# Loading the second query block's mixed heads ahead of the last pair's split

## The chip, the cores and the metric

The kernel runs on one core of a Trainium2 chip. A core has five engines with instruction streams of their own: TensorE (PE in the profile, with its weight loads as PEld), VectorE (DVE), ScalarE (ACT), GpSimd (POOL) and SyncE (SP), which here issues nearly all DMAs. The engines meet only at semaphores. The metric is the device time of one execution in microseconds, the median of several runs.

## The reference

The kernel computes one layer of an encoder over 2048 positions of width 1024 (in float32; `forgetting_attention` is a causal softmax over q k plus c[t] - c[s]):

```
h = rms_norm(x, norm_mix_g)
z = h @ w_in
out_a = spatial_gating(u_a, v_a, ...)             # 8 gMLP heads of 64, blocks of 128 positions
out_b = forgetting_attention(q_b, k_b, v_b, f)    # 8 attention heads of 64
x = x + concat([out_a, out_b]) @ w_out
x = x + conv_ffn(rms_norm(x), w_up, w_conv, b_conv, w_down)
out = rms_norm(x, norm_final_g)
```

What matters here is the third line from the bottom: the product with `w_out` needs, for each position, the 512 columns of the gMLP heads and the 512 columns of the attention heads. Together they are called the mixed heads.

## The kernel before, in words

Every large matmul is made of three: operands are split into a high part and a low remainder (hi, lo), and `mm3` (L210, its matmul is L216) adds hi x hi, hi x lo and lo x hi over 8 chunks of 128, 24 matmuls for one output tile of 128 x 512. In c_half the mixed heads are the stationary operand (`thi`, `tlo` in the profile) and `w_out` the moving one (`whi`, `wlo`), so these matmuls are listed as `mm<-whi,thi`, `mm<-wlo,thi` and `mm<-whi,tlo`.

The positions are worked on in four query blocks of 512 (0 to 3), two in each half of the sequence. Phase A (`a_half`) makes the projections and the gMLP heads and writes the transposed results to memory (`mixh`, `mixl`, one pair of arrays per block, rows 0 to 511). `c_half` multiplies the mixed heads of blocks 0 and 1 (its b = 0 and b = 1) with `w_out` and adds x; `d_half` is the first half of the feed-forward part; `c_late` and what follows do the same for blocks 2 and 3.

The attention is a filler that runs beside all of this. `b_stream` (L730) is a Python generator over 32 pieces, (head h, block tb), block by block. Every matmul of `mm3` counts a tick, and every few ticks `step` (L117) gives out the next small portion of the filler, with a priority 100 places ahead of its place in the program (AHEAD_B). `need(tb)` (L138) gives out portions until all pieces of the blocks up to tb are out. A piece is `b_max` (scores for the row maximum, L829 with the reductions L832 and L834 on DVE), then `b_mix` (scores again, L877 and L881, exponentials, product with the values, L865 and L866). After each second head `b_mix` divides the pair's output by the row sums (matmuls L916, four transposes L190 into a PSUM tile of tag `s`, product L923 into the tile `op`), splits it (`split_sb`: hi on ACT, L203, lo on DVE, L204) and writes it to rows 512 to 1023 of `mixh` and `mixl`, 128 rows for a pair. The scores and these transposes share the three PSUM tiles of tag `s` (`scores`, L787).

The mixed heads of a block are read back with `load_mix` (L936) into tiles of 4 chunks each: the first holds chunks 0 to 3 (the gMLP heads), the second chunks 4 to 7 (the attention pairs). Each load brings two chunks, 512 KB, hi and lo by turns. For block 1 there is one exception: the last pair, head 7 with tb = 1, is not written to memory but split straight into chunk 7 of the tiles (L925, L926). For that, `b_mix` gets the tiles itself with `parts(1)` (L172). `load_mix` then gets them as `given` and loads only chunk 6 in its last step (256 KB).

In `c_half` (L945) the order of the program for b = 0 is: four loads of x (`acc`), the weights and the four output tiles of column half 0, then `need(1)`, then `load_mix(1, self.mix1)`, which on SyncE comes behind the last `acc` load (`issue_after`), then the weights and output tiles of column half 1. Then comes b = 1 with the mixed heads of block 1.

Pieces with tb of 2 or more are held back until `self.ready` is set, since their inputs come late; before the change this happens in `run` (L1580), just ahead of `c_half`.

What order the engines get is not the program's: a planner (a list scheduler with its own model of time) places each instruction when its inputs and its buffer are there, by priority. Buffers come from pools, a fixed number per tag (`BUFS`: two `thi` and two `tlo` tiles per pool, one `op`, three `s`).

Of the kernel before, what the change touches and what calls it, by code (L numbers as in the profile page):

```python
# [33 lines left out]
AHEAD_B, AHEAD_W = 100, 2000  # L34
# [20 lines left out]
def f32(ap):  # L55
    return ap.bitcast(F32)
# [26 lines left out]
class Block:  # L83
# [51 lines left out]
    def start_fill(self, gen, rate):  # L135
        self.fill, self.rate, self.credit = gen, rate, 0.0

    def need(self, tb):  # L138

        while self.done < 8 * (tb + 1):  # L140
            self.step()
            self.count += 3
            while self.late and self.late[0][0] <= self.count:
                self.late.pop(0)[2]()
# [709 lines left out]
    def b_mix(self, h, tb, t1, turn):  # L854

        nc, bp, pp = self.nc, self.bp, self.bpp
        t2 = self.b_low(h, tb)
        po = self.til(pp, [P, TB], F32, "o")
        total = self.room([P, TB], F32, "sum")
        ns = 4 * tb + 4  # L860
        late = []

        def pv():
            sc, c, v, ph, pl = late.pop(0)
            nc.tensor.matmul(po[:, c], lhsT=v, rhs=ph[:, c], start=sc == 0, stop=False)  # L865
            nc.tensor.matmul(po[:, c], lhsT=v, rhs=pl[:, c], start=False, stop=sc == ns - 1)  # L866

        for sc in range(ns):
            if sc == TURN and turn:
                turn()  # L870
            if sc % 4 == 0:
                m1, m2, v4 = self.b_keys(h, sc // 4, True)
            j = max(0, sc - 4 * tb)
            c = slice(j * P, TB)
            ks = slice((sc % 4) * P, (sc % 4 + 1) * P)
            ps = self.scores([P, TB])
            nc.tensor.matmul(ps[:, c], lhsT=m1[:, ks], rhs=t1[:, c], start=True, stop=False)  # L877
            if sc >= 4 * tb and not tb:
                nc.tensor.matmul(ps[:, j * P:(j + 1) * P], lhsT=self.same, rhs=self.maskT, start=False, stop=False,
                                 skip_group_check=True)  # L880
            nc.tensor.matmul(ps[:, c], lhsT=m2[:, ks], rhs=t2[:, c], start=False, stop=True)  # L881
            if sc >= 4 * tb and tb:
                d = ps[:, j * P:(j + 1) * P]
                nc.vector.tensor_tensor(d, d, self.maskT, op=ALU.add)
            e = self.room([P, TB], F32, "e") if sc else total
            nc.scalar.activation(e[:, c], ps[:, c], AF.Exp, scale=-1.0)  # L886
            if len(late) >= (LAG + 1 if self.more else LAG):
                pv()
            ph = self.room([P, TB], F32R, "ph")
            pl = self.room([P, TB], F32R, "pl")  # L890
            nc.scalar.activation(ph[:, c], e[:, c], AF.Copy)  # L891
            nc.vector.tensor_tensor(pl[:, c], e[:, c], f32(ph[:, c]), op=ALU.subtract)  # L892
            if sc:
                nc.vector.tensor_tensor(total[:, c], total[:, c], e[:, c], op=ALU.add)  # L894
            late.append((sc, c, v4[:, sc % 4, :], ph, pl))
            yield
        while late:
            pv()
            yield

        if h % 2 == 0:
            self.op = self.til(self.mp, [P, TB], F32, "op")
            self.fold = self.til(self.mp, [P, TB], F32, "rw")
        op, fold = self.op, self.fold
        own, other = (slice(0, 64), slice(64, 128)) if h % 2 == 0 else (slice(64, 128), slice(0, 64))
        nc.scalar.activation(op[own, :], po[other, :], AF.Copy)
        nc.vector.tensor_tensor(op[own, :], po[own, :], op[own, :], op=ALU.add)
        nc.scalar.activation(fold[own, :], total[other, :], AF.Copy)
        nc.vector.tensor_tensor(fold[own, :], fold[own, :], total[own, :], op=ALU.add)
        if h % 2 == 0:  # L910
            return

        yield
        ps = self.scores([P, 4, 2])
        for i in range(4):
            nc.tensor.matmul(ps[:, i, :], lhsT=fold[:, i * P:(i + 1) * P], rhs=self.pair, start=True, stop=True)  # L916
        rr = self.til(bp, [P, 4, 2], F32, "rr")
        nc.vector.reciprocal(rr, ps)
        rw = self.til(self.mp, [P, 4, 2, 64], F32, "rw")
        nc.scalar.activation(rw, rr.unsqueeze(3).broadcast_to([P, 4, 2, 64]), AF.Copy)  # L920
        yield
        pr = self.transpose4(None, "s", [rw[:, i, :, :].rearrange("p a b -> p (a b)") for i in range(4)])
        nc.vector.tensor_tensor(op, pr, op, op=ALU.mult)  # L923
        if h == 7 and tb == 1:
            self.mix1 = self.parts(1)  # L925
            self.split_sb(op, *[part[:, 7, :] for part in self.mix1])  # L926
            return
        oh = self.room([P, TB], F32R, "ph")
        ol = self.room([P, TB], F32R, "pl")
        self.split_sb(op, oh, ol)  # L930
        cs = slice(512 + (h - 1) * 64, 512 + (h + 1) * 64)
        self.dma(self.mixh[tb][cs, :], f32(oh))
        self.dma(self.mixl[tb][cs, :], f32(ol))
# [11 lines left out]
    def c_half(self, half, accp):  # L945
        nc, pp = self.nc, self.dpp
        mix = [self.mix0, None]
        for b in range(2):
            mh, ml = mix[b]
            rows, acc = [], []  # L950
            for t in range(4 * b, 4 * b + 4):
                x = self.til(accp, [P, D], F32, "acc")
                t0 = half * HALF + t * P
                acc_ins = self.dma(x, self.a["x"][0, t0:t0 + P, :]).ins
                acc.append(x)
            for col in (b, 1 - b):
                if b == 0 and col == 1:
                    self.need(2 * half + 1)
                    with self.tc.issue_after(acc_ins):
                        mix[1] = self.load_mix(1, self.mix1)  # L960
                cs = slice(col * 512, (col + 1) * 512)
                if b == 0 or col == 0:
                    us = [self.load_unit(self.a["w_out"][4 * col + j], 512) for j in range(4)]
                    wh = [us[k // 2][0][:, k % 2, :] for k in range(KC)]
                    wl = [us[k // 2][1][:, k % 2, :] for k in range(KC)]
                for t in range(4):
                    ts = slice(t * P, (t + 1) * P)
                    ps = self.til(pp, [P, TB], F32, "mm")
                    self.mm3(ps, [mh[:, k, ts] for k in range(KC)], [ml[:, k, ts] for k in range(KC)], wh, wl)
                    ac = acc[t]  # L970
                    nc.vector.tensor_tensor(ac[:, cs], ps, ac[:, cs], op=ALU.add)
                    if col == 1 - b:
                        self.dma(self.rows_d[half][4 * b + t], ac)
                        row = self.til(self.rowp, [P, D], F32, "ar")
                        r = self.row_scale(self.dp, ac, row)
                        nc.gpsimd.tensor_scalar(row, ac, r, 0.0, ALU.mult, ALU.add)
                        rows.append(row)
            hi, lo = self.hT[b] = self.parts(b)

            def turn(c, rows=rows, hi=hi, lo=lo):  # L980
                self.transpose_split(pp, "dn", [r[:, c * P:(c + 1) * P] for r in rows],
                                     self.g_ffn[:, c:c + 1], hi[:, c, :], lo[:, c, :])

            for c in range(KC):
                self.defer(26 + 8 * c, lambda c=c, turn=turn: turn(c))
# [574 lines left out]
    def run(self):  # L1560
# [16 lines left out]
        self.dp = dstack.enter_context(tc.tile_pool(name="dpool", bufs=1, reuse_waits="tile"))  # L1577
        self.accs, self.bxs = ExitStack(), ExitStack()
        self.rowp = self.accs.enter_context(tc.tile_pool(name="rowp", bufs=1, reuse_waits="tile"))
        self.ready = True  # L1580
        self.rate = RATES[2]
        self.c_half(0, accp)
        self.rate = RATES[3]
# [51 lines left out]
```

## Time and profile before

| | us |
|---|---|
| median of 3 runs | 2375.96 (2373.01 to 2376.89) |
| the profiled execution | 2374.53 |
| its span, first to last instruction | 2372.8 |
| granted TensorE clock, mean | 0.998 |

The page's second part cuts the span in 40 slices of 59.3 us and gives the busy share of each in tenths:

```profile
PE   9999999999899999999999999999999999999998
DVE  7458777876679888999899986698888887866875
DMA  6763625568645444444444474222222238438633
```

TensorE shows 9 nearly everywhere. The one 8 in the middle, the eleventh slice, is 593 to 652 us, in which `c_half` lies. Busy means here that some matmul was in the array; since matmuls overlap (a matmul of 512 columns is listed with some 0.39 us and the next one begins 0.23 us later), a full slice doesn't say that the array ran at its best rate. The rows to read are therefore the idle times that stand in square brackets behind an instruction, with what ended them, and the distance between starts.

In the timelines a line is: start in us, duration, engine, line of the kernel, operation, output<-inputs, partitions and elements, count. For DMA issues on SyncE (SPq) the duration is that of issuing, not of the transfer. `x2` means that two issues in a row are shown as one.

### The profile page before, as it was taken

Reading aid. Unit: us, or ns where it says so; the run is one execution under the profiler, and the core shown is the slowest. Engines: PE = TensorE matmul, PEld = TensorE weight load, DVE = VectorE, ACT = ScalarE, POOL = GpSimd, SP = SyncE. Lnnn points to the kernel's source line nnn. Section 1 sums busy time; section 2 is a strip of 40 time slices with the busy share of each in tenths; the row PEclk is TensorE's granted clock in tenths of the full one; section 3 lists DMA queues with packets and bytes.
Section 4 is the critical chain, followed back from the end, with each engine's and each line's share of the span. In section 5 each row is a group of like instructions: output and inputs, shape, how many; then the busy total and the mean of one; then the engine's idle time right before and its main releaser. Section 6 shows DMA issues by size and latency. Waiting matters only on the chain.

```text
span 2372.8 us, 32085 instructions
## 1 busy us (share of the span) xinstructions
PE 2348.2 (99%) x11144; PEld 1957.7 (83%) x11144; DVE 1883.7 (79%) x3146; ACT 1215.6 (51%) x2189; POOL 281.3 (12%) x278
## 2 busy tenths in 40 slices
PE   9999999999899999999999999999999999999998
PEld 7988888988787888888888888788888888888887
DVE  7458777876679888999899986698888887866875
ACT  4346646533436555656566654555545555454444
POOL 4114140100223111111100101100000000000001
PEclk9999999999999999999999999999999999999999
DMA  6763625568645444444444474222222238438633
GB/s 213 197 227 113 191 87 168 156 191 269 219 144 205 165 149 143 148 164 165 150 146 149 151 244 147 93 71 80 80 81 98 80 133 292 147 124 291 199 114 125
DMA packets 232818, 374.29 MB, mean 158 GB/s; under 512 B 49784, under 2 KB 109304, under 8 KB 231232
## 3 DMA queue, kind: packets, MB, share of 16 engines
q1 hardware_dynamic: 227616, 348.12, 45.5%
q0 software_dynamic: 5040, 24.12, 2.6%
q8 instruction: 88, 1.44, 0.2%
q14 instruction: 74, 0.61, 0.1%
HBM read 279.10 MB, written 93.20 MB: 157 GB/s over the span
## 4 chain that ended last, share of the span: by engine, by line
PE 91%; DVE 4%; DMA 2%; issue 1%; ACT 1%; POOL 1%; SPq 0%; POOLq 0%; DVEq 0%; ACTq 0%
PE mm L216 43%; PE D L1449 15%; PE A L1247 3%; PE A L1249 3%; PE A L1248 3%; PE o L866 3%; PE o L865 3%; PE s L881 2%; PE s L877 2%; PE s L829 2%; PE B L1248 2%; PE B L1249 2%; PE B L1247 2%; PE C L1247 1%; PE C L1248 1%
## 5 line engine op out<-in xcount | busy, mean ns | idle before, releaser
L216 PE MATMUL mm<-thi,whi 128*128 128x512 f32 x896 | 351.4, 392 | 1.2 <-DVE vn L538 1.2
L216 PE MATMUL mm<-thi,wlo 128*128 128x512 f32 x896 | 351.8, 393 | 0.0
L216 PE MATMUL mm<-tlo,whi 128*128 128x512 f32 x896 | 351.8, 393 | 0.0
L216 PE MATMUL mm<-whi,thi 128*128 128x512 f32 (+2 forms) x768 | 275.5, 359 | 6.4 <-DMA thi<-mixh 5.0
L216 PE MATMUL mm<-wlo,thi 128*128 128x512 f32 (+2 forms) x768 | 274.7, 358 | 0.0
L216 PE MATMUL mm<-whi,tlo 128*128 128x512 f32 (+2 forms) x768 | 273.7, 357 | 0.0
L216 PEld LDWEIGHTS mm<-thi,whi 128*128 128x128 f32 x896 | 168.6, 188 | 36.0 <-POOL whi L152 1.1
L216 PEld LDWEIGHTS mm<-tlo,whi 128*128 128x128 f32 x896 | 168.5, 188 | 34.5
L216 PEld LDWEIGHTS mm<-thi,wlo 128*128 128x128 f32 x896 | 168.6, 188 | 34.1
L216 PEld LDWEIGHTS mm<-whi,thi 128*128 128x128 f32 x768 | 144.9, 189 | 26.5 <-DMA thi<-mixh 5.3
L169 DVE TENSOR_TENSOR wlo<-raw,whi 128x1024 fp32r<-128x1024 f32 (+2 forms) x106 | 132.5, 1250 | 40.1 <-POOL whi L152 24.6
L216 PEld LDWEIGHTS mm<-wlo,thi 128*128 128x128 f32 x768 | 145.0, 189 | 19.3
L216 PEld LDWEIGHTS mm<-whi,tlo 128*128 128x128 f32 x768 | 144.6, 188 | 19.4
L886 ACT ACTIVATE e<-s 128x512 f32<-128x512 f32 (+3 forms) x204 | 104.0, 521 | 90.9 <-PE s L881 50.2
L1006 DVE SCALAR_TENSOR_TENSOR t<-a,cols,t 128x512 f32<-128x512 f32 (+2 forms) x176 | 139.4, 792 | 11.7 <-ACT t L1000 10.9
L1449 PE MATMUL D<-wl,xh 128*128 128x512 f32 x368 | 141.3, 389 | 0.0
L1449 PE MATMUL D<-wh,xh 128*128 128x512 f32 x368 | 140.8, 389 | 0.2 <-DVE xo L1550 0.2
L1449 PE MATMUL D<-wh,xl 128*128 128x512 f32 x368 | 137.5, 389 | 0.0
L152 POOL TENSOR_SCALAR whi<-raw 128x1024 fp32r<-128x1024 f32 (+3 forms) x70 | 79.9, 1144 | 484.7 <-PE mm L216 360.7
L894 DVE TENSOR_TENSOR sum<-sum,e 128x512 f32<-128x512 f32 (+3 forms) x189 | 119.5, 632 | 17.1 <-ACT e L886 15.7
L892 DVE TENSOR_TENSOR pl<-e,ph 128x512 fp32r<-128x512 f32 (+3 forms) x189 | 115.4, 616 | 12.5 <-PE o L866 10.6
L891 ACT ACTIVATE ph<-e 128x512 fp32r<-128x512 f32 (+3 forms) x189 | 101.8, 548 | 28.4 <-PE o L865 13.7
(1931 smaller groups left out, 5749.0 us busy)
## 6 DMA issues: line engine op xcount, KB each, us to landing
raw<-in_w_up_dram SPq DMA_DIRECT2D x72, 512.0 KB
x<-act SPq DMA_DIRECT2D x84, 256.0 KB
m<-kx SPq DMA_DIRECT2D x67, 256.0 KB
v<-vd SPq DMA_DIRECT2D x67, 256.0 KB
m<-kx SPq DMA_DIRECT2D x119, 136.0 KB
raw<-in_w_in_dram SPq DMA_DIRECT2D x28, 512.0 KB
raw<-in_w_out_dram SPq DMA_DIRECT2D x24, 512.0 KB
tw<-in_w_down_dram SPq DMA_DIRECT2D x11, 1024.0 KB
```

What stands on the lines that cost most here:

```text
L152: self.cast_ins = self.nc.gpsimd.tensor_scalar(out, in_, 1.0, 0.0, ALU.mult, ALU.add).ins
L169: nc.vector.tensor_tensor(lo, raw, f32(hi), op=ALU.subtract)
L216: self.last_mm = self.nc.tensor.matmul(ps, lhsT=a[k], rhs=b[k], start=i == 0, stop=i == 3 * n - 1).ins
L886: nc.scalar.activation(e[:, c], ps[:, c], AF.Exp, scale=-1.0)
L891: nc.scalar.activation(ph[:, c], e[:, c], AF.Copy)
L892: nc.vector.tensor_tensor(pl[:, c], e[:, c], f32(ph[:, c]), op=ALU.subtract)
L894: nc.vector.tensor_tensor(total[:, c], total[:, c], e[:, c], op=ALU.add)
L1006: nc.vector.scalar_tensor_tensor(t[:, c], a[:, n + c.start:n + TB], cw[:, cc], t[:, c], op0=ALU.mult, op1=ALU.add)
L1247: mm(ps, lhsT=xh[:, ks], rhs=yh[:, k, :], start=fresh and k == 0, stop=False, **kw)
L1248: mm(ps, lhsT=xh[:, ks], rhs=yl[:, k, :], start=False, stop=False, **kw)
L1249: mm(ps, lhsT=xl[:, ks], rhs=yh[:, k, :], start=False, stop=k == 3, **kw)
L1449: nc.tensor.matmul(bank[t], lhsT=x[i][:, ts], rhs=w[k], start=fresh and j == 0 and i + k == 0, stop=last and i == 1, **kw)
```

## The change

`need` takes a second argument, how many pieces may still be missing. The last pair of block 1 no longer gets tiles and splits; it leaves a function, `last_pair`, that does the split into tiles given later. `c_half` gets the tiles and loads the other chunks at its start (behind the `acc` loads, after `need(1, 2)`, which leaves out the last two pieces). Where it loaded them before, it now gives out the split, with the filler's priority, and sets `ready`, which `run` no longer sets. So the pieces of block 2 are held back until that place.

```diff
-    def need(self, tb):
+    def need(self, tb, left=0):
 
-        while self.done < 8 * (tb + 1):
+        while self.done < 8 * (tb + 1) - left:
...
         if h == 7 and tb == 1:
-            self.mix1 = self.parts(1)
-            self.split_sb(op, *[part[:, 7, :] for part in self.mix1])
+            self.last_pair = lambda parts: self.split_sb(op, *[part[:, 7, :] for part in parts])
             return
...
+            if not b:
+                self.need(1, 2)
+                with self.tc.issue_after(acc_ins):
+                    mix[1] = self.load_mix(1, self.parts(1))
             for col in (b, 1 - b):
                 if b == 0 and col == 1:
-                    self.need(2 * half + 1)
-                    with self.tc.issue_after(acc_ins):
-                        mix[1] = self.load_mix(1, self.mix1)
+                    self.need(1)
+                    with self.tc.high_priority(AHEAD_B):
+                        self.last_pair(mix[1])
+                    self.ready = True
...
-        self.ready = True
         self.rate = RATES[2]
         self.c_half(0, accp)
```

## The prediction

> **What bounds the kernel now.** I began with the page's first part, then the waits of TensorE (PE), then the groups by line.
>
> ```profile
> PE 2348.2 (99%) x11144; PEld 1957.7 (83%) x11144; DVE 1883.7 (79%) x3146; ACT 1215.6 (51%) x2189; POOL 281.3 (12%) x278
> ```
> ```profile
> PE mm L216 <- DMA thi<-mixh: 5.0, 1, 5.0
> ```
>
> TensorE is busy 99% of the span, so time can only come from its own work, which this change leaves alone, or from the few places where it stands still. The second fence is the longest of these: one wait of 5.0 us, of a matmul of `mm3` (L216) for a load of mixed heads. I looked for its place in TensorE's timeline (start, us, line, out<-in, idle before).
>
> ```profile
> 633.71 0.82 PE L190 MATMUL dn<-ident,ar 128*128 128x128 f32 x6
> 634.37 0.60 PE L190 MATMUL s<-ident,rw 128*128 128x128 f32 x4
> 634.72 0.71 PE L829 MATMUL s<-m,t 96*128 96x512 f32 x2
> 636.11 0.49 PE L829 MATMUL s<-m,t 96*128 96x512 f32 x1 [0.67 <-DVE part L832]
> 636.92 1.01 PE L829 MATMUL s<-m,t 96*128 96x512 f32 x2 [0.32 <-DVE op L923]
> 638.16 0.96 PE L829 MATMUL s<-m,t 96*128 96x512 f32 x2
> 644.13 0.79 PE L216 MATMUL mm<-whi,thi 128*128 128x512 f32 x1 [5.01 <-DMA thi<-mixh]
> 646.00 0.63 PE L829 MATMUL s<-m,t 96*128 96x512 f32 x1
> 648.12 0.48 PE L216 MATMUL mm<-whi,tlo 128*128 128x512 f32 x1
> ```
>
> The 192 matmuls of b=0 in `c_half` (8 groups of 24) end before 633.71. The matmul at 644.13 is the first of b=1. Between them stand only transposes and the first scores of the third query block (L829). Then I read the same place in stretches (us, engines, granted clock, DMA share, GB/s).
>
> ```profile
> 633.70:639.10 5.40, 4.33 (x20) 2.39 (x18) 5.10 (x9) 2.83 (x6) 1.86 (x3) 1.00 0.59 185
> 639.10:644.10 5.00, 0.02 (x1) 0.00 (x0) 3.18 (x6) 0.50 (x1) 0.00 (x0) 0.69 1.01 376
> 644.10:648.10 4.00, 3.97 (x15) 3.38 (x16) 1.16 (x4) 0.58 (x1) 0.00 (x0) 0.54 1.05 343
> ```
>
> The granted clock falls to 0.69 in the wait and is 0.54 for 4.0 us behind it, so the wait costs more than its 5.0 us.
>
> What the matmul waits for stands in SyncE's timeline, in the chain of waits, and in two lists of DMA issues (584 to 590 us, then 637 to 641).
>
> ```profile
> 585.51 0.43 SPq L102 DMA_DIRECT2D thi<-mixh  x1
> 588.08 0.57 SPq L102 DMA_DIRECT2D tlo<-mixl  x1
> 592.32 7.71 SPq L102 DMA_DIRECT2D m<-kx  x3
> 637.20 1.72 SPq L102 DMA_DIRECT2D thi<-mixh  x2
> 639.47 1.13 SPq L102 DMA_DIRECT2D tlo<-mixl  x2
> ```
> ```profile
> 637.20 6.89 DMA thi<-mixh
> ```
> ```profile
> thi<-mixh SPq DMA_DIRECT2D x1, 512.0 KB
> thi<-mixh SPq DMA_DIRECT2D x1, 256.0 KB
> ```
> ```profile
> thi<-mixh SPq DMA_DIRECT2D x2, 512.0 KB
> ```
>
> The 256 KB piece is chunk 6 alone (`n = 1`), so the issues at 585 to 588 fill the second tile (chunks 4 to 6), and those at 637 to 640 the first (chunks 0 to 3). Chunks 0 to 3 are the gMLP heads, whose writes to memory end soon after 402 us (all 16, with first and last start):
>
> ```profile
> L102 SPq DMA_DIRECT2D mixh<-st x16: 359/374/492, 232.1 to 402.1; - x16
> ```
>
> They are late for another reason, which the next rows show (ACT, then DVE).
>
> ```profile
> 636.81 0.63 ACT L203 ACTIVATE thi<-op 128x512 fp32r<-128x512 f32 x1 [1.02 <-DVE op L923]
> ```
> ```profile
> 638.48 0.68 DVE L204 TENSOR_TENSOR tlo<-op,thi 128x512 fp32r<-128x512 f32 x1
> ```
>
> These are the last pair's split. The `thi` loads follow its ACT half by 0.39 us, the `tlo` loads its DVE half (ends 639.16) by 0.31. In program order the split is the first to write the second tile of each tag, and the load only later writes the first one. I read the rows so: the planner hands out a tag's tiles in program order of first use, so the first tile's loads are placed behind the split.
>
> **The change, part by part.** *The loads ahead of the split.* `parts(1)` and the loads now come ahead in program order, behind the four `acc` loads. So nothing holds chunks 0 to 3 any more, if their buffer is free:
>
> ```profile
> 575.10 0.39 PE L216 MATMUL mm<-thi,wlo 128*128 128x512 f32 x1
> ```
>
> This is phase A's last matmul out of that pool, ten us before the first load. So I put the four late issues at about 588.7, behind 588.08 + 0.57. On SyncE they take at most 1.72 + 1.13 = 2.85 us and pass only the `m<-kx` issue at 592.32, with 3.7 us free ahead of it: nothing is lost there. The DMA engines are another matter:
>
> ```profile
> 590.00:595.00 5.00, 5.00 (x24) 4.06 (x23) 4.68 (x8) 1.86 (x4) 0.00 (x0) 1.00 1.04 406
> 595.00:601.00 6.00, 6.00 (x31) 5.08 (x30) 5.04 (x9) 2.32 (x5) 1.42 (x2) 1.00 0.25 88
> ```
>
> They are full up to 595 at 406 GB/s. Four loads of 512 KB are 2.1 MB, 5.2 us at that rate; the next stretch has 0.75 x 6.0 = 4.5 us free. They spill over by 0.7 us and land by about 602, 32 us before b=1 needs them. At worst (no gap used) the attention filler's own loads land 5.2 us late; at best nothing moves. I take nothing, as the second row is the nearest.
>
> The Trainium skill (DMA: Bandwidth & Descriptors, Specifications) gives an HBM limit of about 358 GB/s per core and speaks against this cover: 2.1 MB would take 5.9 us and spill 1.4. The 406 GB/s of this trace is above that figure, so the measurement decides.
>
> *What is saved.* I count what TensorE did from 633.71 to 648.12, 14.41 us, and price it at full clock by rows of the chain of waits and two rows of the groups in this stretch:
>
> ```profile
> L829 PE MATMUL s<-m,t 96*128 96x512 f32 x8 | 3.8, 494 | 1.0 <-DVE part L832 0.7 <-DVE op L923 0.3
> L190 PE MATMUL dn<-ident,ar 128*128 128x128 f32 x16 | 3.0, 315 | 0.0
> ```
> ```profile
> 565.44 5.50 PE mm L216 x24
> 570.94 0.44 PE s L190 x4
> 571.38 0.47 PE s L829 x2
> ```
>
> Four L216 at 5.50/24 = 0.229 make 0.92; 16 + 4 transposes at 0.11 make 2.20; eight full L829 at 0.235 make 1.88, and two narrow ones (128 and 256 columns) some 0.2. Work 5.2, so **9.2 us are lost**: 5.01 + 0.67 + 0.32 = 6.0 in waits, the other 3.2 in the slow stretch and in issue.
>
> *The split behind the loads.* It adds a write behind landed loads: by 602 against 636.81, no wait. Behind it on ACT and DVE stand the transposed rows of b=0 (L199, L200), as now. What is late next is chunk 7: its low half is ready at 639.16. Even if TensorE goes straight to b=1 after the ten L190 at 633.71 (1.1 us), it reaches chunk 7 after 21 matmuls, 633.71 + 1.1 + 4.8 = 639.6. Cost nothing; if the filler is 5.2 us late, 4.8 us.
>
> *The third block waits.* `ready` is set 96 matmuls later in the program, so its pieces are given out later. This adds no semaphore. Its first scores (634.72) come behind the last pair's transposes (634.37), which use the same PSUM tag `s`, when all 192 matmuls of b=0 are done. So the later place already lies ahead of its execution: cost 0, with 96 x 0.229 = 22.0 us as the other end if the planner keeps the full distance. Below zero there is no gain, since it only moves work back.
>
> *The far end.* The last block's mixed heads are loaded as the filler ends. Timeline of SyncE, then the chain:
>
> ```profile
> 1473.04 0.37 SPq L102 DMA_DIRECT2D tlo<-mixl  x1
> ```
> ```profile
> 1481.12 1.83 PE mm L216 x8
> ```
>
> With the 6.89 us of the earlier load it lands at 1479.9 (an estimate). The first low-half matmul behind the transposes starts at about 1481, so the slack is some 1.0 us. The main work now arrives 9.2 us sooner. The filler gains too, since it stood behind the blocked matmul:
>
> ```profile
> 646.67 0.69 DVE L832 TENSOR_REDUCE part<-s 128x1 f32<-128x512 f32 x1 [4.39 <-PE s L829]
> ```
>
> DVE waited 4.39 us for the filler's next score. If the filler gains only that, the far end gives back 9.2 - 4.4 - 1.0 = 3.8 us; if it follows the main work, nothing. I take 1.3, nearer to nothing, because filler and main work share all engines and what is freed on DVE also speeds the filler.
>
> Sum: -9.2 + 1.3 = **-7.9 us**. The profiled execution took 2374.53 us (span 2372.8 and 1.7 around it), so 2366.6. The median of the runs, 2375.96, is 1.43 above that: **2368.1 us**.
>
> **The rivals.** *R1, the filler is late.* The moved loads hold up the filler's loads by 5.2 us, the split comes 4.8 us too late and b=1 waits for chunk 7. With about 2.0 us of slow clock behind it (4.0 us at 0.54 lose 1.8), 9.2 - 4.8 - 2.0 = 2.4 are saved: 2373.6. For it: DMA share 1.04 at 590. Against it: the 0.25 of the next row, and a second group's 21 matmuls that could run meanwhile.
>
> The Trainium skill (TensorE: Matmul & The Clock Gate, Part 1) says that an idle window of about 3.4 us halves the clock. The 0.69 and 0.54 above agree; by that rule R1's wait still pays for the slow stretch, and one under 3.4 us would not.
>
> *R2, given back at the far end.* The filler moves up by nothing: 9.2 - 1.0 = 8.2 are lost again at the last block, 2375.0. For it: the slack there is small. Against it: the 4.39.
>
> *R3, nothing changes.* The loads keep their place for a reason not seen, 2376.0. Against it: the free buffer, and the second tile's loads at 585.
>
> *R4, slower.* The third block really starts later, by d. Its end, and with it the load at 1473, moves back by d, and the last block waits: time = 2368.1 + d. From d = 7.9 the gain is gone. At the full 22.0, with 1.8 of slow clock, it is 2391.9. For it: the small slack at 1473. Against it: the order at 634.37 and 634.72.
>
> **How the numbers follow.** Forecast 0.65 (own range 2364 to 2371: the full 9.2, less 3 for the spread of the runs, and the 3.8 given back); R1 0.07; R2 0.10; R3 0.06; R4 0.12. The program is planned anew behind 585 us, which no row prices; it widens both ends. Range 2363.0 to 2376.5: it holds the forecast, R1, R2 and R3, 0.88, less 0.06 for tails. A measurement of this kernel can tell about 0.2%, 4.75 us, from no change. The forecast is faster (0.65), and a little of R1 and R2 (0.02); the rest of R1, R2 and R3 with the small d of R4 is the same (0.22); R4 beyond d = 12.7 slower (0.11).
>
> **What would show it.** Right: all `thi<-mixh` issues of this block below 592 us, no PE wait for `thi<-mixh` in the list of waits, granted clock 1.00 near 640, and the first L829 of the third block still behind the four transposes into `s`. R1: the split later than 640 us and a wait for `thi` or `tlo` from ACT or DVE. R2 and R4: a new wait of TensorE for `mixh` or `mixl` near 1470. Wrong altogether: the issues still at 637.

## The result, and the profile after

| | before | after |
|---|---|---|
| median, us | 2375.47 (6 runs, 2373.01 to 2376.89) | 2365.67 (6 runs, 2364.31 to 2368.37) |
| ratio | | 0.9959, 95% interval 0.9948 to 0.9969 |
| profiled execution, us | 2374.53 | 2365.29 |
| its span, us | 2372.8 | 2363.6 |

The change saves 9.8 us between the medians and 9.2 us between the spans; 2368.1 was predicted. The first part of the page and the longest of TensorE's waits, both after:

```profile
PE 2346.7 (99%) x11144; PEld 1957.6 (83%) x11144; DVE 1875.6 (79%) x3146; ACT 1216.0 (51%) x2189; POOL 282.3 (12%) x278
```
```profile
PE A L1251 <- ACT t2h L1092: 1.8, 1, 1.8
```

The wait for `thi<-mixh`, 5.0 us and the longest before, is gone from the list; the longest is now one of 1.8 us at another place (L1251). SyncE's timeline after shows the loads of block 1:

```profile
584.29 0.43 SPq L102 DMA_DIRECT2D thi<-mixh  x1
...
586.41 1.39 SPq L102 DMA_DIRECT2D thi<-mixh  x1
...
588.58 0.52 SPq L102 DMA_DIRECT2D thi<-mixh  x1
...
590.00 0.33 SPq L102 DMA_DIRECT2D thi<-mixh  x1
591.27 0.36 SPq L102 DMA_DIRECT2D tlo<-mixl  x1
592.57 5.95 SPq L102 DMA_DIRECT2D m<-kx  x3
```

All four `thi` loads stand ahead of 592 us, and the issue of `m<-kx` behind them has moved by 0.25 us (592.32 before). The same stretches of TensorE as in the prediction, and the two in which the loads were to fit (us, engines, granted clock, DMA share, GB/s), after:

```profile
595.00:601.00 6.00, 6.00 (x31) 5.08 (x30) 5.58 (x10) 2.09 (x5) 2.90 (x2) 1.00 0.96 351
601.00:606.00 5.00, 5.00 (x24) 4.17 (x23) 3.76 (x7) 1.36 (x3) 0.11 (x1) 1.00 0.91 290
633.70:639.10 5.40, 5.40 (x28) 4.44 (x28) 1.75 (x3) 0.99 (x3) 1.85 (x3) 1.00 0.61 179
639.10:644.10 5.00, 5.00 (x26) 4.08 (x25) 3.64 (x7) 1.38 (x2) 0.00 (x0) 1.00 0.69 224
644.10:648.10 4.00, 4.00 (x23) 3.38 (x22) 3.19 (x6) 1.36 (x2) 0.00 (x0) 1.00 0.42 156
```

From 633.70 to 648.10 TensorE is busy throughout, at full clock, with 28 + 26 + 23 = 77 instructions where before it had 20 + 1 + 15 = 36. The DMA gap at 595 is filled (0.96 where it was 0.25), and 601 to 606 is full as it was (0.91; 0.93 before).

So far this looks like a forecast that came out by its own reasons. The experiments show that it did so only in part: two of its steps failed, in opposite directions.

### The profile page after: what moved, and what is told of

Read it like the earlier page. It is cut to its first block, busy times and chain, and to the rows that moved or that the text cites. A ratio compares the mean times of both kernels' runs of the same rounds, so it can differ in the third digit from the quotient of the medians.

```text
span 2363.6 us, 32066 instructions
## 1 busy us (share of the span) xinstructions
PE 2346.7 (99%) x11144; PEld 1957.6 (83%) x11144; DVE 1875.6 (79%) x3146; ACT 1216.0 (51%) x2189; POOL 282.3 (12%) x278
## 4 chain that ended last, share of the span: by engine, by line
PE 83%; DVE 3%; DMA 2%; ACT 1%; issue 1%; POOL 0%; SPq 0%; POOLq 0%; DVEq 0%; ACTq 0%
PE mm L216 37%; PE D L1453 14%; PE A L1251 3%; PE A L1252 3%; PE A L1253 3%; PE o L866 3%; PE o L865 3%; PE s L881 2%; PE s L877 2%; PE s L829 2%; PE B L1253 2%; PE B L1252 2%; PE B L1251 2%; PE C L1252 1%; PE C L1253 1%
## 5 line engine op out<-in xcount | busy, mean ns | idle before, releaser
L216 PE MATMUL mm<-thi,whi 128*128 128x512 f32 x896 | 351.4, 392 | 0.5 <-DVE vn L538 0.5
L216 PE MATMUL mm<-thi,wlo 128*128 128x512 f32 x896 | 351.9, 393 | 0.0
L216 PE MATMUL mm<-tlo,whi 128*128 128x512 f32 x896 | 351.4, 392 | 0.0
L216 PE MATMUL mm<-whi,thi 128*128 128x512 f32 (+2 forms) x768 | 274.8, 359 | 2.3 <-DVE fs L536 1.4
L216 PE MATMUL mm<-wlo,thi 128*128 128x512 f32 (+2 forms) x768 | 274.4, 357 | 0.0
L216 PE MATMUL mm<-whi,tlo 128*128 128x512 f32 (+2 forms) x768 | 274.1, 357 | 0.0
L216 PEld LDWEIGHTS mm<-thi,whi 128*128 128x128 f32 x896 | 168.5, 188 | 35.0 <-issue 1.0
L216 PEld LDWEIGHTS mm<-thi,wlo 128*128 128x128 f32 x896 | 168.5, 188 | 34.7
L216 PEld LDWEIGHTS mm<-tlo,whi 128*128 128x128 f32 x896 | 168.5, 188 | 34.0
L216 PEld LDWEIGHTS mm<-whi,thi 128*128 128x128 f32 x768 | 144.7, 188 | 22.2 <-issue 1.5
L216 PEld LDWEIGHTS mm<-whi,tlo 128*128 128x128 f32 x768 | 144.6, 188 | 19.4
L216 PEld LDWEIGHTS mm<-wlo,thi 128*128 128x128 f32 x768 | 144.8, 188 | 19.2
L892 DVE TENSOR_TENSOR pl<-e,ph 128x512 fp32r<-128x512 f32 (+3 forms) x183 | 110.4, 607 | 20.8 <-PE o L866 10.9
L891 ACT ACTIVATE ph<-e 128x512 fp32r<-128x512 f32 (+3 forms) x183 | 98.4, 545 | 31.3 <-PE o L865 18.2
```

Source lines behind the costliest of these rows:

```text
L216: self.last_mm = self.nc.tensor.matmul(ps, lhsT=a[k], rhs=b[k], start=i == 0, stop=i == 3 * n - 1).ins
```

## The experiments

The question was which half of the edit makes the gain. Kernel 1 is that of experiment 1, and so on. The program of the third block matters for the answer, so here is the part that the prediction passed over. In `d_half`, behind its first two units, the kernel sets `self.more`. From that place in the program the filler has additional buffers (tags with a "+": `ph+`, `pl+`, `e+`, `m1+` and others), may put its scores also into PSUM tiles of tag `dn`, lets its products with the values lag one step more, and is given out woven: the scores of one head between the mixing steps of the head before it. From there ACT also makes the weights' casts, which GpSimd made before (L165). The place is fixed in the program, but how far the filler has come there depends on when `ready` was set.

### 1 and 2: each half alone

The loads ahead of the split, but the third block given out as early as before:

```diff
                     with self.tc.high_priority(AHEAD_B):
                         self.last_pair(mix[1])
-                    self.ready = True
...
+        self.ready = True
         self.rate = RATES[2]
         self.c_half(0, accp)
```

> The changed kernel, but with the third block's pieces given out as early as before the change (ready is set ahead of c_half); only the loads are moved. My theory (the whole gain is the wait for thi<-mixh with its slow stretch, and holding the third block back costs and gains nothing): as the changed kernel, 2365.7 us, within 2; chunks 0 to 3 loaded between 584 and 592 us, no wait of TensorE for thi<-mixh. Rival (the gain, or part of it, comes from holding the third block back): 2370 to 2375. Second rival (holding it back costs something that the gain covers): below 2363.

Measured: 2375.76 us, ratio to before 1.0000 (0.9991 to 1.0008). The loads alone gain nothing. The wait near 640 is gone in its profile too. In its place stands another, in the list of waits, in SyncE's timeline and in the stretches of the far end:

```profile
PE mm L216 <- DMA thi<-mixh: 6.4, 1, 6.4
```
```profile
1467.01 0.33 SPq L102 DMA_DIRECT2D mixh<-ph+_3176_13680  x1
...
1469.04 0.37 SPq L102 DMA_DIRECT2D thi<-mixh  x1
```
```profile
1465.00:1475.00 10.00, 3.62 (x13) 2.44 (x12) 2.68 (x4) 8.65 (x13) 3.48 (x8) 0.74 0.58 205
```

The last block's mixed heads are written at 1467.01, when the filler ends, and loaded at 1469.04. That is where they were before (1469.89), while the main work now arrives earlier. TensorE works for 3.62 of 10 us there, and the clock is down to 0.74. In the time nothing is left of the gain.

The other half alone: the kernel before, with only `ready` set later.

```diff
                     with self.tc.issue_after(acc_ins):
                         mix[1] = self.load_mix(1, self.mix1)
+                    self.ready = True
...
-        self.ready = True
```

> The kernel before, with only ready set at col 1 of b=0, behind the loads; the loads stay behind the split. My theory: as before, 2375.5 us within 2; the thi<-mixh loads still near 637 us and TensorE still waits about 5.0 us for them with a granted clock near 0.7 and 0.55 behind it. Rival (the third block's later pieces make the gain): about 2366 to 2370.

Measured: 2373.50 us, ratio 0.9992 (0.9983 to 1.0001). The loads stand behind the split again (SyncE), and the wait is back (3.4 us in this profile):

```profile
635.68 1.41 SPq L102 DMA_DIRECT2D thi<-mixh  x2
```
```profile
PE mm L216 <- DMA thi<-mixh: 3.4, 1, 3.4
```

The first half alone is worth nothing, the second some 2 us, which the interval doesn't tell from nothing; together they are worth 10.

### 3 and 4: why the loads were late

The split given out ahead of the loads, both 96 matmuls earlier than in the kernel before:

```diff
             if not b:
-                self.need(1, 2)
+                self.need(1)
+                mix[1] = self.parts(1)
+                with self.tc.high_priority(AHEAD_B):
+                    self.last_pair(mix[1])
                 with self.tc.issue_after(acc_ins):
-                    mix[1] = self.load_mix(1, self.parts(1))
+                    self.load_mix(1, mix[1])
```

> The changed kernel, but at the start of c_half the last pair's split is given out ahead of the loads instead of behind them; both stand 96 matmuls earlier in the program than in the kernel before, and ready is set as in the changed kernel. My theory (tiles of a tag are handed out in program order of first use, and the split writes the second tile first): the loads of chunks 0 to 3 are placed behind the split again, near 637 us, TensorE waits about 5 us for thi<-mixh, and the time is 2374 to 2376 us. Rival (what counts is only how early the loads stand in the program): loads between 584 and 592 us, no wait, 2365 to 2368.

Measured: 2375.36 us, ratio 0.9998 (0.9989 to 1.0007); TensorE waits 3.8 us for `thi<-mixh`. SyncE's timeline:

```profile
587.58 0.43 SPq L102 DMA_DIRECT2D thi<-mixh  x1
...
637.51 1.51 SPq L102 DMA_DIRECT2D thi<-mixh  x2
```

An early place in the program doesn't help; two of the four loads are behind the split. Then only the load of chunks 0 and 1 ahead of the split, the others behind it:

```diff
-                    mix[1] = self.load_mix(1, self.parts(1))
+                    self.load_mix(1, mix[1], (0,))
+                with self.tc.high_priority(AHEAD_B):
+                    self.last_pair(mix[1])
+                with self.tc.issue_after(acc_ins):
+                    self.load_mix(1, mix[1], (2, 4, 6))
```

> The changed kernel, but only the load of chunks 0 and 1 stands ahead of the split; the loads of chunks 2 and 3 and of 4 to 6 stand behind it in the program. My theory (the first load opens the first tile of each tag, and behind that no load waits for the split): all four thi loads between 584 and 592 us, no wait of TensorE for thi<-mixh, 2365 to 2368 us. Rival (each load that stands behind the split in the program is placed behind it): chunks 2 to 6 are loaded near 637 us, TensorE runs 12 matmuls of the first group (2.8 us) and then waits about 2 to 4 us, 2371 to 2375.

Measured: 2365.48 us, ratio 0.9956 (0.9942 to 0.9969), as the changed kernel. The loads on SyncE:

```profile
585.60 0.64 SPq L102 DMA_DIRECT2D thi<-mixh  x1
...
591.84 0.33 SPq L102 DMA_DIRECT2D thi<-mixh  x1
```

The first pair of loads (hi and lo of chunks 0 and 1) ahead of the split is enough: it opens the first tile of each tag. This part of the prediction's reading held.

### 5 and 6: is it the woven form?

In the changed kernel the piece of head 5 in the third block falls behind the place where `more` is set, and is woven; with `ready` early it isn't. My second theory was that this form makes the filler faster. The changed kernel without that weaving:

```diff
-            if todo and (self.more or tb == 0):
+            if todo and (self.more and (h, tb) != (5, 2) or tb == 0):
```

> The changed kernel, but the piece of head 5 in the third block keeps the form it has in the kernel before: its scores are given out in one run ahead of the mixing of head 4 instead of woven into it. The loads stay ahead of the split. My theory (holding the third block back by 97 matmuls puts this piece behind the place in d_half where weaving and more buffers begin, and the woven form is what makes the filler 10 to 16 us faster, so that nothing is given back at the far end): the fifth head's scores start some 9 us later than in the changed kernel, the last mixed heads are written near 1464 to 1470 us, TensorE waits for the load of mixed heads near 1465 again, and the time is 2371 to 2376 us. Rival (the later start of the third block as such keeps the gain, whatever the form of that piece): 2365 to 2367.

Measured: 2366.43 us, ratio 0.9962 (0.9950 to 0.9975). The theory fell by the time, though not by every sign: the last mixed heads are written at 1463.08 (1457.69 in the changed kernel, whose profile stands 1.7 us earlier from 585 on), so the filler is some 4 us slower, and TensorE waits 1.3 us for their loads. In this profile the wait at L1251 is 0.3 us instead of 1.8, which hides part of that in the time. So the form is a part of the filler's gain, not the 10 to 16 us. Its converse, kernel 1 with that piece woven:

```diff
-            if todo and (self.more or tb == 0):
+            if todo and (self.more or tb == 0 or (h, tb) == (5, 2)):
```

> The first experiment's kernel (loads ahead of the split, third block given out early as before the change), with one edit: the piece of head 5 in the third block is woven into the mixing of head 4, as in the changed kernel, but still without the additional buffers, which come later in the program. My theory: the filler gains most of the 10 to 16 us, the last mixed heads are written near 1452 to 1460 us, and the time is 2364 to 2368 us, with the third block early. Rival (only the later start keeps the gain): as the first experiment, 2374 to 2377, with a wait of about 6 us near 1466.

Measured: 2378.19 us, ratio 1.0012 (1.0003 to 1.0020), with 7.1 us of waiting for `thi<-mixh` at the far end. Without the buffers the form makes the filler no faster: the last mixed heads are written at 1469.95, against 1467.01 in kernel 1, whose profile stands 3.2 us earlier from 585 on.

### 7 and 8: holding the third block longer

`ready` another 96 matmuls later, at the start of b=1, and then only behind `c_half`:

```diff
-                    self.ready = True
...
+            self.ready = b == 1
             if not b:
                 self.need(1, 2)
```

> The changed kernel with ready set another 96 matmuls later, at the start of b=1 of c_half. By the program the same pieces are woven as in the changed kernel (from head 5 on), but the third block starts up to 22 us later. My theory (the later start has a price of its own at the far end, which the changed kernel doesn't pay because it weaves one piece more): the third block's first scores near 655 us, the last mixed heads are written 5 to 20 us later than in the changed kernel, TensorE waits for them near 1460, time 2370 to 2382. Rival (my step on record: a later place in the program costs nothing): 2365 to 2367.

Measured: 2362.33 us (2361.75 to 2362.49), ratio 0.9942 (0.9930 to 0.9954): the fastest kernel of the study, 3.3 us below the changed one, against both of the outcomes I had written down.

```diff
-                    self.ready = True
...
         self.c_half(0, accp)
+        self.ready = True
```

> The changed kernel with ready set only behind c_half, 288 matmuls (66 us at 0.229) later in the program. Two pieces more are woven than in the changed kernel (from head 3 on). My theory: the start is 60 us later, two woven pieces win back 20 to 32 us, and the main work that is no longer interrupted runs ahead, so the last mixed heads come 20 to 45 us after TensorE needs them: 2385 to 2410 us. Rival (a later place costs nothing): 2365 to 2367. Second rival (each woven piece pays for the delay): 2360 to 2370.

Measured: 2363.99 us, ratio 0.9951 (0.9938 to 0.9965). My theory had 20 us of loss and more; only the second rival's range, that the pieces behind the place of `more` pay for the delay, holds the time. For `ready` at b=1 the next fences show that the start doesn't move: the third block's first scores in TensorE's timeline of the changed kernel, then of the kernel with `ready` at b=1.

```profile
636.71 0.60 PE L190 MATMUL s<-ident,rw 128*128 128x128 f32 x4
637.07 0.71 PE L829 MATMUL s<-m,t 96*128 96x512 f32 x2
```
```profile
636.78 0.71 PE L829 MATMUL s<-m,t 96*128 96x512 f32 x2
```

96 matmuls later in the program, the third block starts at the same time. In kernel 8 it does start later, at 643.91. In both the filler ends sooner all the same. The mixed heads of the third block's pairs are written three times between 650 and 1000 us; a row each (count, duration, first and last start) for before, kernel 1, the changed kernel and `ready` at b=1:

```profile
L102 SPq DMA_DIRECT2D mixh<-ph x3: 319/320/327, 777.2 to 990.7; - x3
```
```profile
L102 SPq DMA_DIRECT2D mixh<-ph x3: 320/332/338, 778.3 to 993.3; - x3
```
```profile
L102 SPq DMA_DIRECT2D mixh<-ph x3: 326/327/332, 779.1 to 978.0; - x3
```
```profile
L102 SPq DMA_DIRECT2D mixh<-ph x3: 326/327/333, 779.4 to 962.6; - x3
```

The first pair is written within 2.2 us of the same time in all four. The third pair is written at 990.7 and 993.3 where `ready` is early, at 978.0 where it is 96 matmuls later, and at 962.6 where it is 192 later. Some 15 us are gained with each step, between 780 and 990 us, long after the start.

The second of these steps isn't what makes kernel 7 faster than the changed kernel. In neither does TensorE wait for mixed heads at the far end (last `thi` load at 1442.08 and 1460.02). But at L1251, near 1530, the changed kernel waits 1.8 us for ACT, with a slow clock behind it, and kernel 7 0.4 us, without. Kernel 7's wait, then the 2 us behind it in the changed kernel and in kernel 7 (granted clock behind the engines):

```profile
PE A L1251 <- ACT t2h L1092: 0.4, 1, 0.4
```
```profile
1532.00:1534.00 2.00, 2.00 (x6) 1.51 (x6) 2.00 (x2) 0.25 (x2) 0.00 (x0) 0.50 0.00 0
```
```profile
1530.00:1532.00 2.00, 2.00 (x10) 1.65 (x10) 2.00 (x2) 0.80 (x2) 0.00 (x0) 1.00 0.00 0
```

That is 1.4 us less of waiting and some 1.7 us less of slow clock (an estimate: 3.4 us at 0.50), about the 3.3 us between the two kernels. Why ACT is late there in the one and not in the other wasn't traced.

### 9 and 10: how much is given out with the few buffers

That led to a third theory: what counts is how many of the third block's pieces are given out behind the place of `more`. The changed kernel, with the filler's use of `more` (buffers and weaving, not the weights' casts) 96 matmuls later:

```diff
-        if self.more and n % (BUFS[tag] + BUFS[tag + "+"]) >= BUFS[tag]:
+        if self.wide and n % (BUFS[tag] + BUFS[tag + "+"]) >= BUFS[tag]:
...
+                self.defer(96, lambda: setattr(self, "wide", True))
```

> The changed kernel (loads ahead, third block held), but the filler gets its additional buffers and the woven form 96 matmuls later in the program, so as many of its pieces are given out with the few buffers as in the kernel before; the weights' casts change engine where they did. New theory (what counts is how much of the third block is given out behind the place where the additional buffers begin; holding the block back by 96 matmuls shifts 96 matmuls' worth of it into the many buffers, where it runs faster): the first score into the tag dn comes near 925 to 935 us instead of 896, the last mixed heads are written near 1464 to 1470, TensorE waits 3 to 7 us for their load, and the time is 2371 to 2377 us. Rival (the later place of the third block as such keeps the gain): 2365 to 2367, last write near 1458.

Measured: 2375.20 us, ratio 0.9998 (0.9989 to 1.0006). The gain is gone, with the loads ahead and the third block held as in the changed kernel. The third pair's write is late again, and the last mixed heads come at 1470.38:

```profile
L102 SPq DMA_DIRECT2D mixh<-ph x3: 320/332/339, 780.3 to 999.9; - x3
```
```profile
PE mm L216 <- DMA thi<-mixh: 7.3, 1, 7.3
```

The converse: kernel 1, third block early, but the filler pauses for the first 96 matmuls of `d_half`, ahead of the place of `more`:

```diff
             ws = [units(f0), units(f0 + 1)]
+            if not f0:
+                held, self.fill = self.fill, None
             for k in range(2):
                 self.d_up(f0 + k, *ws[k], 0)
+            if not f0:
+                self.fill = held
```

> The first experiment's kernel (loads ahead of the split, third block given out as early as before the change), but the filler gives out nothing during the first 96 matmuls of d_half, which lie ahead of the place where the additional buffers begin. New theory (how much is given out ahead of that place): the same pieces have the additional buffers as in the changed kernel, the first score into dn comes near 890 to 900 us instead of 933, the last write near 1455 to 1460, no wait over 1 us at the far end, 2363 to 2368 us. Rival (the later start of the third block as such): as the first experiment, 2374 to 2377, with the wait near 1466.

Measured: 2365.71 us, ratio 0.9955 (0.9942 to 0.9969): the changed kernel's time to a tenth, with `ready` where it was before. Its third pair:

```profile
L102 SPq DMA_DIRECT2D mixh<-ph x3: 326/326/332, 781.2 to 981.5; - x3
```

Both came out within a microsecond of the ranges that the theory gave, and against "the later start as such". The place at which the filler gets its first score into `dn` moves along: by rows of L877 it is at 935.3 in kernel 9 and 898.4 in kernel 10. The group rows of L881 for kernel 1, then the changed kernel:

```profile
L881 PE MATMUL dn<-t,m x2: 221/278/335, 933.5 to 933.9; 128*128 128x256 f32 x1, 128*128 128x128 f32 x1
```
```profile
L881 PE MATMUL dn<-t,m x8: 389/389/396, 896.0 to 918.7; 128*128 128x512 f32 x8
```

Which of the things that begin at this place does it was not tried, but for the weaving of one piece (5 and 6). ACT's waits for a free `ph` are in the right direction but small: from 650 to 1000 us, 9.4 us in kernel 1 and, with `ready` at b=1, 5.5 for `ph` and 2.2 for `ph+` (L891, ended by the products of L865). They don't make up 30 us of difference by themselves.

### 11 and 12: the limits

`ready` only in `d_half`, where the buffers begin, so that the whole third block has them:

```diff
                 self.more = True
+                self.ready = True
```

> The changed kernel with ready set only in d_half, where the additional buffers begin: the whole third block is given out with them, 480 matmuls (110 us) later in the program than in the changed kernel. New theory (more buffers against a later start): the third block's first scores can only come once the rest has let go, near 715 us, some 70 us later than in the kernel that had ready behind c_half, and only the three pieces it had ahead of the buffers are faster; so the last mixed heads come 10 to 40 us later than its 1445.5, and the time is 2362 to 2385 us, above the 2362.3 of ready at b=1. Rival (the later the better): 2358 to 2362. My step on record with its other end (the later place costs all of its distance): above 2400.

Measured: 2364.50 us, ratio 0.9959 (0.9947 to 0.9972), as expected above the 2362.3. Holding longer than to b=1 wins nothing more, and costs some 2 us.

And the place that was best, without moving the loads (the kernel before, `ready` at the start of b=1):

```diff
             mh, ml = mix[b]
+            self.ready = b == 1
...
-        self.ready = True
```

> The kernel before (loads of chunks 0 to 3 still behind the split), with ready set at the start of b=1, the place that gave 2362.3 us with the loads moved. It prices the loads where the far end has slack. My theory (the loads are worth the 9.2 us of the wait and its slow stretch, and they come through in full once the filler is ahead): the wait for thi<-mixh near 640 us is back, no wait at the far end, 2369 to 2373 us. Rival (with the filler well ahead the wait near 640 costs little, because other work moves into it): 2362 to 2366.

Measured: 2374.47 us, ratio 0.9997 (0.9988 to 1.0006). The kernel with the loads ahead gave 2362.33, so the loads are worth 12.1 us here. I had expected 6.7 to 10.7. The wait is back, though only 2.0 us of it:

```profile
PE mm L216 <- DMA thi<-mixh: 2.0, 1, 2.0
```

The place still costs what it did before. The matmuls of L216 from 630 to 655 us, in the kernel before, in kernel 12 and in kernel 7 (PE, PEld, granted clock, DMA share, GB/s):

```profile
630.00:655.00 25.00, 11.45 (x41) 7.63 (x41) 0.86 0.65 217
```
```profile
630.00:655.00 25.00, 12.01 (x40) 8.69 (x40) 0.80 0.53 175
```
```profile
630.00:655.00 25.00, 20.68 (x81) 14.51 (x80) 1.00 0.43 132
```

TensorE's other instructions there number 48, 53 and 51. So kernel 12 is 41 matmuls behind kernel 7, some 9.4 us at 0.229 (an estimate), and the kernel before 40, some 9.2. What makes up the other 2.7 us of the 12.1 wasn't traced.

The six kernels in which only the two halves differ, in us:

| | `ready` ahead of `c_half` | at col 1 | at b=1 |
|---|---|---|---|
| loads behind the split | 2375.5 (before) | 2373.5 | 2374.5 |
| loads ahead | 2375.8 | 2365.7 (after) | 2362.3 |

Neither the loads alone nor a later `ready` alone gains more than 2.3 us, counted from the medians beside them. There are two limits in parallel: the main work, late by the wait near 640 us, and the filler, which must end before the last block's mixed heads can be loaded. Removing one lets the other decide. In kernels 2 and 12 the filler is early, with the last mixed heads written at 1446.12 and 1441.19 (1467.78 before), and the main work still late by the wait.

## Why the prediction was right, and where it was not

The number was right (2368.1 forecast, 2365.67 measured, inside the forecast's own range of 2364 to 2371). Step by step:

- **What bounds the kernel, and why the loads were late: right.** Order of tiles by first use was a reading of timelines; kernels 3 and 4 separate it from its rivals.
- **The DMA cover: right.** From 595 to 601 the DMA engines move 351 GB/s instead of 88, some 1.6 of the 2.1 MB. From 601 to 606 they were nearly full before as well and move 290 GB/s instead of 273, so no spill beyond the 0.7 us shows. TensorE is busy for all 11.00 us of these two stretches, so it cost nothing. The row of 601 to 606 before:

```profile
601.00:606.00 5.00, 5.00 (x24) 4.16 (x23) 4.90 (x8) 1.64 (x4) 1.65 (x1) 1.00 0.93 273
```

- **9.2 us saved near 640: borne out.** The matmuls of L216 from 630 to 655 us, 41 before and 81 in kernel 7, price it at some 9.2 us. In time, moving the loads is worth 7.8 us with `ready` at col 1 (2373.5 to 2365.7) and 12.1 with it at b=1, once the far end has room.
- **The split behind the loads: right.** ACT's half starts at 638.07 (636.81 before) and DVE's ends at 639.83 (639.16), and b=1 doesn't wait. The rows of ACT and DVE after:

```profile
638.07 0.63 ACT L203 ACTIVATE thi<-op 128x512 fp32r<-128x512 f32 x1 [4.01 <-DVE op L923]
```
```profile
639.15 0.68 DVE L204 TENSOR_TENSOR tlo<-op,thi 128x512 fp32r<-128x512 f32 x1
```

- **"The third block waits: cost 0 ... Below zero there is no gain, since it only moves work back": this step failed.** Between kernel 1 and the changed kernel the start indeed doesn't move: the scores come right behind the four transposes into `s` in both (635.76 and 637.07, in profiles that stand 1.5 us apart from 585 on). R4, which priced a later start at its full delay, is refuted by kernel 8: its scores come 6.8 us later than the changed kernel's, and it is no slower. But with the loads ahead, holding the block back is worth 10.1 us (2375.8 to 2365.7). It changes which of its pieces are given out with additional buffers, and the priced row, the start at 634, doesn't show that. `self.more` is in the code, and no term of the sum asked for it.
- **The far end, 1.3 us given back: this step failed too.** For the loads alone the filler moves up by nothing: its last load stands at 1469.04 against 1469.89, and TensorE waits 6.4 us. The 4.39 us that DVE got back near 646 didn't reach the filler's end. That is R2 within a microsecond (2375.0 worked out, 2375.8 measured), to which I gave 0.10; R2 was meant for the whole change, where it didn't come. In the changed kernel the far end gives back almost nothing, because the filler itself became faster:

```profile
1460.02 0.37 SPq L102 DMA_DIRECT2D thi<-mixh  x1
1460.78 0.37 SPq L102 DMA_DIRECT2D tlo<-mixl  x1
```

These loads come 9.9 us earlier than before (1469.89). The two errors, some 8 us too little given back and some 10 us of gain not seen, cancelled but for 2.4 us. That the number came out was luck. The signs named for a right forecast (loads below 592 us, no wait for `thi<-mixh`, clock 1.00 near 640, the scores behind the transposes) all came true and couldn't tell this.

Not all of the 9.2 us between the spans comes from the change. The first `thi` load stands at 585.51 before and 584.29 after, and the loads of x ahead of it, which the change leaves alone, moved by 1.4 (582.21 and 580.79); the start of the first `thi` load lies between 582.77 (kernel 1) and 587.58 (kernel 3) in the profiles of this study. So the comparison goes by the medians.

## What to carry to other kernels

When a wait goes away in a kernel with two streams of work, look up where they meet next and compare how early each arrives: a slack of 1 us there means that the gain needs the other stream to move too, and a term for "it probably follows" deserves a run of its own. A change to when work is given out can alter with which buffers or in which form it is given out; list what the program switches at fixed places, and count how much of the work falls on each side of them. A right total doesn't prove its terms: the two halves, each alone, showed in two runs that both terms were wrong.

## What the runs showed of the hardware

The slow clock doesn't need a long wait. In kernel 12 the longest wait near 640 is 2.0 us. TensorE's timeline there, and then stretches of 2 us (granted clock behind the engines):

```profile
635.35 0.44 PE L190 MATMUL dn<-ident,ar 128*128 128x128 f32 x2 [0.48 <-POOL ar L977]
635.81 1.09 PE L829 MATMUL s<-m,t 96*128 96x512 f32 x2
637.17 1.29 PE L829 MATMUL s<-m,t 96*128 96x512 f32 x2 [0.27 <-PE s L829]
...
642.84 0.80 PE L216 MATMUL mm<-whi,thi 128*128 128x512 f32 x1 [2.00 <-DMA thi<-mixh]
```
```profile
634.00:636.00 2.00, 1.50 (x9) 0.81 (x7) 1.63 (x3) 0.59 (x2) 1.19 (x2) 1.00 0.92 310
636.00:638.00 2.00, 1.55 (x4) 0.61 (x3) 1.97 (x4) 1.61 (x3) 0.00 (x0) 0.95 0.33 83
638.00:640.00 2.00, 1.99 (x8) 1.34 (x8) 2.00 (x4) 0.40 (x1) 0.00 (x0) 0.50 0.89 251
...
646.00:648.00 2.00, 2.00 (x6) 1.52 (x6) 0.34 (x3) 0.00 (x0) 0.00 (x0) 0.50 0.23 84
648.00:650.00 2.00, 2.00 (x13) 1.65 (x12) 0.69 (x3) 0.69 (x1) 0.00 (x0) 0.99 0.00 0
```

The clock is 0.50 from 638 on, ahead of the 2.0 us wait that ends at 642.84, and stays there for ten microseconds. In the 4 us ahead of it TensorE was busy for 1.50 + 1.55 = 3.05, with no wait over 0.6 us. So the shorter wait isn't a cheaper one here: kernel 12 is as far behind from 630 to 655 us as the kernel before with its 5.0. Nor does a wait of one length always bring the slow clock: 1.8 us at L1251 were followed by 0.50 in the changed kernel, while behind the same wait in kernel 4 (L1254 there), which ends at 1532.77, the clock stayed at 1.00:

```profile
1534.00:1536.00 2.00, 2.00 (x11) 1.62 (x10) 2.00 (x2) 0.90 (x4) 0.00 (x0) 1.00 0.00 0
```

The Trainium skill (TensorE: Matmul & The Clock Gate, Part 1) gives one idle window of about 3.4 us as the condition, and the prediction took from it that a wait under 3.4 us wouldn't pay for the slow stretch. This run speaks against that use of the rule: here the clock fell behind a stretch that was thinly used, without any wait of that length.
